# Gathering the tokens of two expert pairs at once, in two fp32r passes of 256 columns, with 19 prefetch buffers

## The chip, the cores and the metric

The kernel runs on one core of a Trainium2 chip. The metric is the device time of one execution in microseconds; the runs of a kernel are summarised by their median. The core has a matrix engine (TensorE, here PE; its weight loads are PEld), a vector engine (VectorE, DVE), a scalar engine (ScalarE, ACT), GpSimd (POOL) and SyncE (SP), which here issues the large loads. Matmuls write to eight accumulator banks of 512 fp32 columns.

## The reference

A transformer block with adaptive normalisation, latent and neighbourhood attention and a hierarchical mixture of experts is followed by a second block (gating, linear attention with decay, convolutional feed-forward). There are 256 tokens of width 1024. What the change touches is the mixture of experts: 16 experts in 4 groups; each token takes the best group and two experts in it. The reference computes all experts densely:

```python
def hierarchical_moe(h, w_rg, b_rg, w_re, b_re, w_gate, w_up, w_down):
    ...
    def one_group(args):
        wg_g, wu_g, wd_g, comb_g = args
        hid = jax.nn.silu(jnp.einsum('td,edf->tef', t, wg_g)) * jnp.einsum('td,edf->tef', t, wu_g)
        return jnp.einsum('tef,efd->td', hid * comb_g[:, :, None], wd_g)
```

with `w_gate` and `w_up` of 1024 x 512 and `w_down` of 512 x 1024 for each expert, all in fp32.

## The kernel before

The first block's attention comes first, then routing, then the expert loop, then the second block. In the expert part each expert takes at most 64 tokens (`CAP`), and two experts make a pair of 128 slots. Routing gives each chosen token a place in its expert; `slots_of(p)` (L984) compares places with slot numbers and makes the 0/1 matrix `SS[p]` (tokens x 128 slots, two halves of 128 tokens). `hT` (L950) is the normalised token matrix, tokens on partitions, written by ACT from the accumulator banks `tks`. `gather(p)` (L1058) multiplies `hT` by `SS[p]` in fp32, one 128-wide block of the model width at a time, into one bank per half of the width; `affine` (L1052) scales and shifts each block into `XE`, alternately on ACT and DVE.

The loop over 8 pairs (L1112) then runs, in this order on PE: the gate projection `pg` (L1121 and L1122, the two experts side by side), the transposes of `SS[p]` and the routing weights into a bank `aux` (L1131, L1133), the up projection `pu`, `combine` of the pair before (L1031 and L1032: its output times `ST` in fp32r, high and low part; DVE adds it to `X` at L1035), the transposes of the gated product (L1155, after DVE's multiply L1150), the gather of the next pair (L1064), and the down projection (L1167, L1168). ACT copies the transposed product back to SBUF (L1156) ahead of the down projection. `ST` (L1135) is the transposed slot matrix, copied by DVE out of `aux` right after the gate projection. PE runs in the order in which the program is written (`MANUAL`); the order on ACT, DVE and POOL is chosen by a planner when the kernel is built, within the dependencies that `follow` adds.

The experts' weights come as 96 chunks of 1 MB (1.0486 million bytes), 12 for a pair, two for each half of gate, up and down. `moe_next` (L831) takes them in order on SP's queue, and `KIND` gives each a buffer in turn: four of `rawp` (0), those of `big` (1), three of `bigB` (2), two of `wp` (3), one of `ho` (4); 21 in all. A load past the 21st waits for the matmuls that read the chunk 21 places earlier (`used`). `big` has 13 buffers; `mix` and `YY` take two of them. `mix` holds `XE`, the gated product `sgt` and both slot matrices. `overflow` (L1068) computes the experts again for tokens beyond 64 in an expert, in a conditional branch in the last pair. After the loop the second block's weights (`wC`) are loaded in the same queue, `raw0` first; `pre_high` (L1181) splits it into `wp` buffers.

Of the kernel before, what the change touches and what calls it, by code (L numbers as in the profile page):

```python
# [18 lines left out]
P = 128  # L19
D = 1024  # L20
KD = 8
T = 256
# [96 lines left out]
LAG = 2  # L119
DELAY_FROM = NF - 2  # L120
LASTCUT = 94
KIND = [1] * 9 + [0, 0, 1, 0, 0, 2, 2, 2, 3, 3, 4, 1]
FIRST = "m0 m1 w0 w3"
WARM = 30
EARLY = ("x0 j4 g0 x1 r0 c0 s0 h0 pA g1 j1 c1 h1 pB j3 A0 g2 A1 c2 h2 g3 B0 B1 c3 h3 A2 B2 pC g4 C0 C1 B3 c4 g5 h4 A3 C2 A4 c5 h5 B4 C3 g6 A5 c6 g7 h6 B5 C4 l0 A6 c7 h7 "
# [86 lines left out]
def build(tc, xT, cT, consts, constsA, constsZ, vec, wmod, wA, relb, wE, wC, sgw, sgb, sgln, gfin, out, dbg=None):  # L212
# [10 lines left out]
    with ExitStack() as top:  # L223
# [46 lines left out]
        def bank():  # L270
            return psp.tile([P, 512], F32, name=nm_("b"), tag="b")
# [7 lines left out]
        def follow(d, e):  # L279
            tc.add_manual_dep(d.ins, e.ins.name, order_only, reason="first things first")  # L280
# [84 lines left out]
        with ExitStack() as sa:  # L365
# [465 lines left out]
            def moe_next():  # L831
                i = moe_q[0]
                moe_q[0] += 1
                n = i - len(KIND)
                kind = KIND[i % len(KIND)]
                if kind == 0:
                    return load(moe_chunk(i), cuts=2 if i >= LASTCUT else 1)
                pl, tag = {1: (big, "raw"), 2: (bigB[-1], "raw"), 3: (wp, "w"), 4: (ho, "tL")}[kind]
                t = pl.tile([P, 2048], F32, name=nm_("raw"), tag=tag)
                for a, b in pieces(2048, 2 if i >= LASTCUT else 1):  # L840
                    d = queue(nc.sync.dma_start(t[:, a:b], moe_chunk(i)[:, a:b]))
                    tc.add_manual_dep(d.ins, (used[n] if n >= 0 else moe_gate[0]).ins.name, complete, reason="prefetch")
                return t
# [30 lines left out]
        br = pool(sb, "br", bufs=2)  # L874
        bigB.append(pool(sb, "bigB", bufs=3))
        mix = bigt([P, 2048], "mix")
        XE = mix[:, :KD * P].rearrange("p (k s) -> p k s", k=KD)
        sgt = mix[:, 1024:1536]
        warm(AF.Sqrt, lexp[0])
        G2 = bp.tile([P, KD], F32, name="G2")  # L880
# [44 lines left out]


        with sb:
            def small(shape, name, dt=F32):
                return bp.tile([P] + shape, dt, name=name)

            def bc(ap_, n):
                return ap_.unsqueeze(len(ap_.shape)).to_broadcast(list(ap_.shape) + [n])
# [14 lines left out]
            nc.vector.tensor_reduce(mx_, L, axis=AX.X, op=OP.max)  # L947
            nc.vector.tensor_sub(L, L, bc(mx_, 4))
            lexp[0] = nc.scalar.activation(ex, L, AF.Exp)
            hT = ho.tile([P, 2, D], F32, name="hT", tag="tH")  # L950
            for g in range(2):
                for b in range(2):
                    follow(nc.scalar.activation(hT[:, b, g * 512:(g + 1) * 512], tks[g, b], AF.Copy, scale=col[:, b:b + 1]), lexp[0])
            e1 = small([2, 5, 4], "e1")
            nc.vector.scalar_tensor_tensor(e1, L, 0.0, prio, op0=OP.is_ge, op1=OP.mult)
            nc.vector.tensor_reduce(mx_, e1, axis=AX.X, op=OP.max)
# [24 lines left out]
            slot = cst("slot")  # L981
            SS = {}

            def slots_of(p):  # L984
                SS[p] = mix[:, 1536 + p % 2 * 256:1792 + p % 2 * 256].rearrange("p (b e s) -> p b e s", b=2, e=2)
                for b in range(2):
                    nc.vector.tensor_tensor(SS[p][:, b], bc(place[:, b, 2 * p:2 * p + 2], CAP),
                                            slot.unsqueeze(1).to_broadcast([P, 2, CAP]), op=OP.is_equal)
                SS[p] = SS[p].rearrange("p b e s -> p b (e s)")

            slots_of(0)
            comb = small([2, 4, 4], "comb")
            nc.vector.tensor_mul(comb, exe, top)
            den = small([2, 5], "den")
# [60 lines left out]
                else:  # L1055
                    nc.scalar.activation(dst, src, AF.Identity, scale=G2[:, k:k + 1], bias=mod2[:, 8 + k:9 + k])

            def gather(p):  # L1058
                for g in range(2):
                    ps = bank()  # L1060
                    for k in range(4):
                        for b in range(2):
                            d = (4 * g + k) * P
                            mm(ps[:, k * P:(k + 1) * P], hT[:, b, d:d + P], SS[p][:, b], start=b == 0, stop=b == 1)  # L1064
                    for k in range(4):
                        affine(XE[:, 4 * g + k], ps[:, k * P:(k + 1) * P], 4 * g + k, k % 2)

            def overflow():  # L1068
                last[0] = None
                with tc.If(n_most > CAP):  # L1070
                    ob, turns = [bank() for _ in range(4)], itertools.count()
                    spare = [bigB[-1].tile([P, 2048], F32, name=f"spare{c}", tag="raw") for c in range(3)]
                    H2f, fw = spare[0].rearrange("p (k t) -> p k t", k=KD), spare[1:]
                    for k in range(KD):
                        ps = ob[next(turns) % 4]
                        for b in range(2):
                            nc.tensor.transpose(ps[:, b * P:(b + 1) * P], hT[:, b, k * P:(k + 1) * P], ident)
                        affine(H2f[:, k], ps[:, :T], k, False)
                    hc = bigt([P, 5, T], "hc")
                    hid, cr = hc[:, 0:4], hc[:, 4]  # L1080
                    with tc.For_i(0, NE, 1) as e:
                        nc.gpsimd.dma_start(cr, ovD[bass.ds(e, 1)].to_broadcast([P, T]))

                        def dload(c):
                            t = fw[c % 2]
                            nc.sync.dma_start(t, wE[bass.ds(e, 1), c].rearrange("o p n -> p (o n)"))
                            return t
                        wg = [dload(0), dload(1)]
                        for f in range(4):
                            pg = ob[next(turns) % 4]  # L1090
                            for k in range(KD):
                                s = slice((k % 4) * 512 + f * P, (k % 4) * 512 + (f + 1) * P)
                                mm(pg[:, :T], wg[k // 4][:, s], H2f[:, k], start=k == 0, stop=k == KD - 1)
                            nc.scalar.activation(hid[:, f], pg[:, :T], AF.Silu)
                        wu = [dload(2), dload(3)]
                        for f in range(4):
                            pu = ob[next(turns) % 4]
                            for k in range(KD):
                                s = slice((k % 4) * 512 + f * P, (k % 4) * 512 + (f + 1) * P)
                                mm(pu[:, :T], wu[k // 4][:, s], H2f[:, k], start=k == 0, stop=k == KD - 1)  # L1100
                            nc.vector.tensor_mul(hid[:, f], hid[:, f], pu[:, :T])
# [10 lines left out]
            for p in range(8):  # L1112
                def pairmm(ps, between=None):
                    for hf in range(2):
                        if hf and between:
                            between()
                        wa, wb = next_pair()
                        for kk in range(4):
                            k = 4 * hf + kk
                            s = slice(kk * 512, (kk + 1) * 512)  # L1120
                            la = mm(ps[0:64], XE[:, k, 0:64], wa[:, s], start=k == 0, stop=k == KD - 1)  # L1121
                            lb = mm(ps[64:128], XE[:, k, 64:128], wb[:, s], start=k == 0, stop=k == KD - 1)  # L1122
                        freed(la, lb)

                if p == 1:
# [2 lines left out]
                pairmm(pg, overflow if p == 7 else None)  # L1128
                aux = bank()
                for b in range(2):  # L1130
                    nc.tensor.transpose(aux[:, b * P:(b + 1) * P], SS[p][:, b], ident)  # L1131
                for b in range(2):
                    mm(aux[:, 256:272], SS[p][:, b], comb[:, b], start=b == 0, stop=b == 1)  # L1133
                ST = br.tile([P, T], F32R, name=f"ST{p}", tag="ST")
                nc.vector.tensor_copy(ST, aux[:, :T])  # L1135
                wt = br.tile([P, 1], F32, name=f"wt{p}", tag="wt")
                nc.vector.tensor_copy(wt[0:64], aux[0:64, 256 + 2 * p:257 + 2 * p])
                nc.vector.tensor_copy(wt[64:128], aux[64:128, 257 + 2 * p:258 + 2 * p])
# [3 lines left out]
                pairmm(pu)  # L1142
                if 0 < p < 7:
                    combine(*pend)
                sg = sgt
                nc.scalar.activation(sg, pg, AF.Silu)
                hd = sgt.rearrange("p (f t) -> p f t", f=4)
# [3 lines left out]
                for hf in range(2):  # L1151
# [2 lines left out]
                    for i in range(2):  # L1154
                        nc.tensor.transpose(pt[:, i * P:(i + 1) * P], hd[:, 2 * hf + i], ident)  # L1155
                    nc.scalar.copy(sg[:, o], pt)  # L1156
                if p < 7:
                    slots_of(p + 1)
                    gather(p + 1)
                pd = [bank(), bank()]  # L1160
                for hf in range(2):
                    wa, wb = next_pair()
# [490 lines left out]
```

## Time and profile before

| | us |
|---|---|
| median of 3 runs | 783.11 (781.49 to 783.50) |
| the profiled execution | 783.37 |
| its span | 781.7 |
| PE busy | 761.0 (97%) |
| DVE busy | 452.0 (58%) |
| ACT busy | 359.1 (46%) |
| POOL busy | 28.2 (4%) |

The span is the time from the first to the last instruction of the profiled execution; all times on the time axis below count from its start. Busy time is the union of an engine's instructions; PE's ends are modelled, so that starts are the better measure of spacing. An idle time is followed by what ended it, after an arrow. An fp32 matmul stands as two rows, an fp32r matmul as one.

### The profile page before, as it was taken

The page shows a single profiled execution, that of the slowest core. Times are in us where ns is not written, and L with a number is a line of the kernel's source. Part 1 is how long each engine was busy: PE and PEld are TensorE (multiplying, and loading weights), DVE is VectorE, ACT ScalarE, POOL GpSimd, SP SyncE. Part 2 cuts the span into 40 slices and gives each one's busy share as a digit, 9 for nine tenths or more (in the row PEclk, how much of TensorE's full clock was granted, in tenths as well). Part 3 has the DMA queues.
Part 4 walks back from the last instruction along what each step waited for, and adds up shares of the span by engine and source line. Part 5 has one row for each costly group of instructions (what it writes and reads, how often), then busy time and mean ns, then how long its engine had stood idle before and what let it go on. Part 6 is the DMA issues. An engine that isn't in the chain of part 4 may idle for free. (4 is left out here: it accounts for less than half of the span.)

```text
span 781.7 us, 12585 instructions
## 1 busy us (share of the span) xinstructions
PE 761.0 (97%) x5036; PEld 562.5 (72%) x5036; DVE 452.0 (58%) x926; ACT 359.1 (46%) x669; POOL 28.2 (4%) x35
## 2 busy tenths in 40 slices
PE   8999998999999999999999999999999999999996
PEld 7678776766789445535535535898899999999995
DVE  3737639865763123313313336887786877777785
ACT  5527345765663211111102106578766655655654
POOL 0001000000001000000000004103000000000000
PEclk9999999999999999999999999999999999999999
DMA  8867646657959899999999927654443555545301
GB/s 355 339 241 151 254 151 240 232 192 270 419 178 353 346 413 421 419 420 420 420 419 419 415 105 270 231 171 153 135 156 134 200 180 213 199 166 212 109 1 54
DMA packets 29343, 198.86 MB, mean 254 GB/s; under 512 B 3457, under 2 KB 3857, under 8 KB 6369
## 3 DMA queue, kind: packets, MB, share of 16 engines
q1 hardware_dynamic: 28224, 194.45, 64.5%
q0 software_dynamic: 1056, 3.56, 2.0%
q8 instruction: 41, 0.67, 0.4%
q14 instruction: 22, 0.17, 0.1%
HBM read 196.94 MB, written 1.06 MB: 253 GB/s over the span
## 5 line engine op out<-in xcount | busy, mean ns | idle before, releaser
L315 DVE TENSOR_TENSOR w<-raw,w 128x1024 fp32r<-128x1024 f32 (+1 forms) x118 | 140.0, 1213 | 31.3 <-ACT w L314 31.0
L314 ACT CAST w<-raw 128x1024 fp32r<-128x1024 f32 (+1 forms) x118 | 116.5, 1029 | 25.0 <-PE b L336 20.8
L1122 PE MATMUL b<-raw,mix 128*64 128x512 f32 x256 | 113.4, 594 | 0.5 <-issue 0.5
L1121 PE MATMUL b<-raw,mix 128*64 128x512 f32 x256 | 113.4, 594 | 0.3 <-PEq L1070 0.3
L334 PE MATMUL b<-fH,w 128*128 128x256 f32 x352 | 98.7, 280 | 0.0
L336 PE MATMUL b<-fH,w 128*128 128x256 f32 x352 | 98.3, 279 | 0.0
L335 PE MATMUL b<-fL,w 128*128 128x256 f32 x352 | 98.3, 279 | 0.0
L1121 PEld LDWEIGHTS b<-raw,mix 128*64 128x64 f32 x256 | 34.1, 137 | 67.0 <-issue 64.9
L334 PEld LDWEIGHTS b<-fH,w 128*128 128x128 f32 x352 | 66.1, 188 | 0.9
L335 PEld LDWEIGHTS b<-fL,w 128*128 128x128 f32 x352 | 65.9, 187 | 0.9
L336 PEld LDWEIGHTS b<-fH,w 128*128 128x128 f32 x352 | 66.1, 188 | 0.0
L1167 PE MATMUL b<-raw,mix 128*64 128x512 f32 x128 | 56.6, 595 | 0.0
L1168 PE MATMUL b<-raw,mix 128*64 128x512 f32 x128 | 56.6, 595 | 0.0
L1576 ACT ACTIVATE a<-t,V 128x256 f32<-128x256 f32 x44 | 26.3, 599 | 39.0 <-DVE t L1575 38.9
L1167 PEld LDWEIGHTS b<-raw,mix 128*64 128x64 f32 x128 | 16.9, 137 | 33.1 <-issue 32.0
L1156 ACT COPY mix<-b 128x256 f32<-128x256 f32 x16 | 5.4, 374 | 73.5 <-PE b L1155 73.3
L1122 PEld LDWEIGHTS b<-raw,mix 128*64 128x64 f32 x256 | 34.2, 137 | 2.8 <-issue 2.8
L1150 DVE SCALAR_TENSOR_TENSOR mix<-mix,wt,b 128x256 f32<-128x256 f32 x16 | 7.0, 477 | 48.4 <-PE b L1122 43.2
L336 PE MATMUL b<-w,mL 128*128 128x512 f32 x88 | 34.7, 395 | 0.0
L335 PE MATMUL b<-w,mH 128*128 128x512 f32 x88 | 34.7, 394 | 0.0
L334 PE MATMUL b<-w,mH 128*128 128x512 f32 x88 | 34.7, 394 | 0.0
L1172 DVE TENSOR_TENSOR YY<-b,YY 128x512 fp32r<-128x512 f32 x16 | 10.9, 689 | 38.9 <-ACT YY L1172 38.3
(429 smaller groups left out, 1702.5 us busy)
## 6 DMA issues: line engine op xcount, KB each, us to landing
raw<-in_wE SPq DMA_DIRECT2D x94, 1024.0 KB, 14.0
raw<-in_wC SPq DMA_DIRECT2D x46, 1024.0 KB, 4.9
raw<-in_wmod SPq DMA_DIRECT2D x24, 1024.0 KB, 6.8
raw<-in_wA SPq DMA_DIRECT2D x13, 1024.0 KB, 5.0
raw<-in_wE SPq DMA_DIRECT2D x4, 512.0 KB, 17.7
raw<-in_wA SPq DMA_DIRECT2D x2, 576.0 KB, 4.7
X<-in_xT SPq DMA_DIRECT2D x1, 1024.0 KB, 5.2
CX<-in_cT SPq DMA_DIRECT2D x1, 1024.0 KB, 7.4
```

The source lines that it names most:

```text
L314: hc = nc.scalar.copy(h[:, : b - a], raw[:, a:b])
L315: after[0] = (on or nc.vector).tensor_sub(l[:, : b - a], raw[:, a:b], h[:, : b - a])
L334: mm(ps, ah, bh, start=start, stop=False)
L335: mm(ps, ah, bl, start=False, stop=False)
L336: mm(ps, al, bh, start=False, stop=stop)
L1121: la = mm(ps[0:64], XE[:, k, 0:64], wa[:, s], start=k == 0, stop=k == KD - 1)
L1122: lb = mm(ps[64:128], XE[:, k, 64:128], wb[:, s], start=k == 0, stop=k == KD - 1)
L1150: nc.vector.scalar_tensor_tensor(sg[:, o], sg[:, o], wt, pu[:, o], op0=OP.mult, op1=OP.mult)
L1167: la = mm(pd[n][0:64], hd[:, f, 0:64], wa[:, s], start=f == 0, stop=f == 3)
L1168: lb = mm(pd[n][64:128], hd[:, f, 64:128], wb[:, s], start=f == 0, stop=f == 3)
L1172: ylast = (nc.scalar.copy(yH[:, o], pd[n]), nc.vector.tensor_sub(yL[:, o], pd[n], yH[:, o]))
L1576: nc.scalar.activation(a, t, AF.Identity, bias=bcv[:, n:n + 1], scale=wcv[:, 2, n:n + 1])
```

## The change

`hT` is replaced by two fp32r tiles: `hTH`, the rounded high part (ACT, as `hT` before), and `hTL`, the remainder, made by four DVE operations behind the first slot matrix; `hTL` takes the `ho` buffer that was a prefetch buffer. `slots_of` makes the matrix of two pairs at once (256 slots) in a tile of its own with one buffer, as fp32r. `gather` runs ahead of the loop and in pairs 1, 3 and 5 only; it multiplies the high and then the low part by 256 slots, into two banks per half of the width. `XE` becomes a tile of its own, twice as wide, in `big`. `ST` has one buffer instead of two, and its copy moves behind `combine`. The small fp32 tiles of routing move into the freed part of `mix`. `KIND` loses its last two entries, and so there are 19 prefetch buffers. In `overflow` the spare buffers come from `big`, and the two parts are added up first.

```diff
-KIND = [1] * 9 + [0, 0, 1, 0, 0, 2, 2, 2, 3, 3, 4, 1]
+KIND = [1] * 9 + [0, 0, 1, 0, 0, 2, 2, 2, 3, 3]
...
-        XE = mix[:, :KD * P].rearrange("p (k s) -> p k s", k=KD)
+        XE = bigt([P, KD, 2 * P], "XE")
...
-            hT = ho.tile([P, 2, D], F32, name="hT", tag="tH")
+            hTH = ho.tile([P, 2, D], F32R, name="hTH", tag="tH")
+            hTL = ho.tile([P, 2, D], F32R, name="hTL", tag="tL")
             for g in range(2):
                 for b in range(2):
-                    follow(nc.scalar.activation(hT[:, b, g * 512:(g + 1) * 512], tks[g, b], AF.Copy, scale=col[:, b:b + 1]), lexp[0])
+                    follow(nc.scalar.activation(hTH[:, b, g * 512:(g + 1) * 512], tks[g, b], AF.Copy, scale=col[:, b:b + 1]), lexp[0])
...
-            def slots_of(p):
-                SS[p] = mix[:, 1536 + p % 2 * 256:1792 + p % 2 * 256].rearrange("p (b e s) -> p b e s", b=2, e=2)
+            def slots_of(pp):
+                st = br.tile([P, 512], F32R, name=f"SS{pp}", tag="SS", bufs=1)
+                SS[pp] = st.bitcast(F32).rearrange("p (b s) -> p b s", b=2), st.rearrange("p (b s) -> p b s", b=2)
                 for b in range(2):
-                    nc.vector.tensor_tensor(SS[p][:, b], bc(place[:, b, 2 * p:2 * p + 2], CAP),
-                                            slot.unsqueeze(1).to_broadcast([P, 2, CAP]), op=OP.is_equal)
-                SS[p] = SS[p].rearrange("p b e s -> p b (e s)")
-
-            slots_of(0)
+                    d = nc.vector.tensor_tensor(SS[pp][1][:, b].rearrange("p (e s) -> p e s", e=4), bc(place[:, b, 4 * pp:4 * pp + 4], CAP),
+                                                slot.unsqueeze(1).to_broadcast([P, 4, CAP]), op=OP.is_equal)
+                return d
+
+            placed = slots_of(0)
+            for g in range(2):
+                for b in range(2):
+                    o = slice(g * 512, (g + 1) * 512)
+                    d = nc.vector.scalar_tensor_tensor(hTL[:, b, o], tks[g, b], col[:, b:b + 1], hTH[:, b, o], op0=OP.mult, op1=OP.subtract)
+                    follow(d, placed)
+                    placed = d
...
-            def gather(p):
+            def gather(pp):
                 for g in range(2):
-                    ps = bank()
-                    for k in range(4):
-                        for b in range(2):
-                            d = (4 * g + k) * P
-                            mm(ps[:, k * P:(k + 1) * P], hT[:, b, d:d + P], SS[p][:, b], start=b == 0, stop=b == 1)
-                    for k in range(4):
-                        affine(XE[:, 4 * g + k], ps[:, k * P:(k + 1) * P], 4 * g + k, k % 2)
+                    pss = [bank(), bank()]
+                    for i, ht in enumerate((hTH, hTL)):
+                        for j in range(4):
+                            for b in range(2):
+                                d = (4 * g + j) * P
+                                mm(pss[j // 2][:, (j % 2) * 256:(j % 2 + 1) * 256], ht[:, b, d:d + P], SS[pp][1][:, b],
+                                   start=i + j % 2 + b == 0, stop=i + j % 2 + b == 3)
+                    for j in range(4):
+                        affine(XE[:, 4 * g + j], pss[j // 2][:, (j % 2) * 256:(j % 2 + 1) * 256], 4 * g + j, j % 2)
...
-                ST = br.tile([P, T], F32R, name=f"ST{p}", tag="ST")
-                nc.vector.tensor_copy(ST, aux[:, :T])
...
                 if 0 < p < 7:
                     combine(*pend)
+                ST = br.tile([P, T], F32R, name=f"ST{p}", tag="ST", bufs=1)
+                nc.vector.tensor_copy(ST, aux[:, :T])
...
-                if p < 7:
-                    slots_of(p + 1)
-                    gather(p + 1)
+                if p % 2 and p < 7:
+                    slots_of(p // 2 + 1)
+                    gather(p // 2 + 1)
```

## Rows read from the trace of the kernel before

**Rows 1.** The page: busy time, share of the span and instructions of PE and PEld.

```profile
PE 761.0 (97%) x5036; PEld 562.5 (72%) x5036; DVE 452.0 (58%) x926; ACT 359.1 (46%) x669; POOL 28.2 (4%) x35
```

**Rows 2.** Windows: stretch, busy time by engine (instructions), PE clock, DMA share, GB/s.

```profile
283.30:311.10 27.80, 27.80 (x157) 13.47 (x158) 8.57 (x25) 4.08 (x9) 0.52 (x1) 1.00 1.01 421
...
422.10:449.80 27.70, 27.70 (x156) 13.36 (x154) 7.63 (x20) 4.24 (x9) 0.00 (x0) 1.00 1.01 416
...
476.90:490.00 13.10, 11.65 (x77) 9.83 (x78) 12.93 (x20) 12.85 (x29) 9.39 (x11) 1.00 0.78 287
```

**Rows 3.** Loads of line 841 at 259 to 260 and at 435.8: starts, landing.

```profile
L841 SPq DMA_DIRECT2D raw<-in_wE x2: 328/352/377, 259.3 to 259.7; - x2
...
DMA to landing us min/median/max: 4.9/6.6/8.4
...
L841 SPq DMA_DIRECT2D raw<-in_wE x1: 328/328/328, 435.8 to 435.8; - x1
...
DMA to landing us min/median/max: 16.0/16.0/16.0
```

**Rows 4.** Timeline of PE, last pair: start, duration, line, operation, tiles, shapes.

```profile
468.89 0.89 PE L1155 MATMUL b<-C,mix 128*128 128x128 f32 x4 [0.64 <-DVE mix L1150]
469.79 0.64 PE L1167 MATMUL b<-raw,mix 128*64 128x512 f32 x1
...
473.27 0.59 PE L1167 MATMUL b<-raw,mix 128*64 128x512 f32 x1
...
476.81 0.38 PE L1031 MATMUL b<-ST,YY 128*128 128x256 f32 x1
```

**Rows 5.** Timeline of PE, pair 0, transposes to down projection.

```profile
271.09 0.89 PE L1155 MATMUL b<-C,mix 128*128 128x128 f32 x4 [0.68 <-DVE mix L1150]
271.82 3.74 PE L1064 MATMUL b<-mix,hT 128*128 128x128 f32 x32
275.49 0.64 PE L1167 MATMUL b<-raw,mix 128*64 128x512 f32 x1
```

**Rows 6.** Timeline of all engines, pair 6, slot copy and combine to down projection.

```profile
429.85 0.43 DVE L1135 CAST ST<-b 128x256 fp32r<-128x256 f32 x1 [6.24 <-PE b L1133]
...
436.76 0.38 PE L1031 MATMUL b<-ST,YY 128*128 128x256 f32 x1
...
437.75 3.22 DVE L1035 SCALAR_TENSOR_TENSOR X<-b,mod,X 128x256 f32<-128x256 f32 x8
...
438.67 0.28 PE L1032 MATMUL b<-ST,YY 128*128 128x256 f32 x1
...
438.78 0.60 PE L1155 MATMUL b<-C,mix 128*128 128x128 f32 x4
...
439.20 0.65 ACT L1156 COPY mix<-b 128x256 f32<-128x256 f32 x2 [9.38 <-PE b L1155]
...
442.89 0.64 PE L1167 MATMUL b<-raw,mix 128*64 128x512 f32 x1
```

**Rows 7.** Timeline of all engines around the gather ahead of the loop.

```profile
247.22 2.40 ACT L953 ACTIVATE hT<-b,colB 128x512 f32<-128x512 f32 x4
...
251.41 0.49 DVE L987 TENSOR_TENSOR mix<-place,C 128x128 f32<-128x128 f32 x2
...
251.85 3.81 PE L1064 MATMUL b<-mix,hT 128*128 128x128 f32 x32 [0.70 <-DVE mix L987]
...
255.59 0.64 PE L1121 MATMUL b<-raw,mix 128*64 128x512 f32 x1
```

**Rows 8.** The page's groups: count, busy us, mean ns, idle before, releaser.

```profile
L1156 ACT COPY mix<-b 128x256 f32<-128x256 f32 x16 | 5.4, 374 | 73.5 <-PE b L1155 73.3
...
L1172 DVE TENSOR_TENSOR YY<-b,YY 128x512 fp32r<-128x512 f32 x16 | 10.9, 689 | 38.9 <-ACT YY L1172 38.3
```

**Rows 9.** Waits from 476.9 to the end: who for whom, us, times, longest.

```profile
ACT w L314 <- PE b L336: 8.5, 7, 1.8
```

More of the change, by code (lines that the diff above doesn't have):

```diff
@@ L837, in moe_next @@
                     return load(moe_chunk(i), cuts=2 if i >= LASTCUT else 1)
-                pl, tag = {1: (big, "raw"), 2: (bigB[-1], "raw"), 3: (wp, "w"), 4: (ho, "tL")}[kind]
+                pl, tag = {1: (big, "raw"), 2: (bigB[-1], "raw"), 3: (wp, "w")}[kind]
                 t = pl.tile([P, 2048], F32, name=nm_("raw"), tag=tag)
@@ L927, in build @@
         with sb:
+            taken = [1536]
             def small(shape, name, dt=F32):
-                return bp.tile([P] + shape, dt, name=name)
+                if dt != F32:
+                    return bp.tile([P] + shape, dt, name=name)
+                taken[0] += math.prod(shape)
+                assert taken[0] <= 2048
+                names = "abc"[:len(shape)]
+                return mix[:, taken[0] - math.prod(shape):taken[0]].rearrange(f"p ({' '.join(names)}) -> p {' '.join(names)}", **dict(zip(names[:-1], shape)))
             def bc(ap_, n):
@@ L1071, in overflow @@
                     ob, turns = [bank() for _ in range(4)], itertools.count()
-                    spare = [bigB[-1].tile([P, 2048], F32, name=f"spare{c}", tag="raw") for c in range(3)]
+                    spare = [bigt([P, 2048], f"spare{c}") for c in range(3)]
                     H2f, fw = spare[0].rearrange("p (k t) -> p k t", k=KD), spare[1:]
+                    hR = fw[0].rearrange("p (b d) -> p b d", b=2)
+                    nc.vector.tensor_add(hR, hTH, hTL)
                     for k in range(KD):
@@ L1076, in overflow @@
                         for b in range(2):
-                            nc.tensor.transpose(ps[:, b * P:(b + 1) * P], hT[:, b, k * P:(k + 1) * P], ident)
+                            nc.tensor.transpose(ps[:, b * P:(b + 1) * P], hR[:, b, k * P:(k + 1) * P], ident)
                         affine(H2f[:, k], ps[:, :T], k, False)
@@ L1112, in build @@
             for p in range(8):
+                x = p % 2 * P
+                ss = SS[p // 2][0][:, :, x:x + P]
                 def pairmm(ps, between=None):
@@ L1120, in pairmm @@
                             s = slice(kk * 512, (kk + 1) * 512)
-                            la = mm(ps[0:64], XE[:, k, 0:64], wa[:, s], start=k == 0, stop=k == KD - 1)
-                            lb = mm(ps[64:128], XE[:, k, 64:128], wb[:, s], start=k == 0, stop=k == KD - 1)
+                            la = mm(ps[0:64], XE[:, k, x:x + 64], wa[:, s], start=k == 0, stop=k == KD - 1)
+                            lb = mm(ps[64:128], XE[:, k, x + 64:x + 128], wb[:, s], start=k == 0, stop=k == KD - 1)
                         freed(la, lb)
@@ L1130, in build @@
                 for b in range(2):
-                    nc.tensor.transpose(aux[:, b * P:(b + 1) * P], SS[p][:, b], ident)
+                    nc.tensor.transpose(aux[:, b * P:(b + 1) * P], ss[:, b], ident)
                 for b in range(2):
-                    mm(aux[:, 256:272], SS[p][:, b], comb[:, b], start=b == 0, stop=b == 1)
-                ST = br.tile([P, T], F32R, name=f"ST{p}", tag="ST")
-                nc.vector.tensor_copy(ST, aux[:, :T])
+                    mm(aux[:, 256:272], ss[:, b], comb[:, b], start=b == 0, stop=b == 1)
                 wt = br.tile([P, 1], F32, name=f"wt{p}", tag="wt")
```

## The prediction

> **What bounds the kernel now.** I read the page first, then the windows by stage, the timeline at the seams of the expert loop, and the loads. TensorE (PE) is busy for 97% of the span [rows 1], so the question is which of its work the change removes and what stands ready to stop it when it is early. The windows show the expert loop: each pair of experts takes 27.7 to 27.8 us with PE busy throughout (pairs 2 to 5 read the same as pairs 1 and 6), and in the same stretches the loads run at a DMA share of 1.00 to 1.01 and 416 to 421 GB/s [rows 2]. Two resources are full at once; which of them ends the stage is read at its end: the last load, issued at 435.8, lands 16.0 us later, at 451.8 [rows 3], and the last half of the last down-projection starts at 473.27 [rows 4]. So the loads lead by 21.5 us there, PE ends the stage, and what PE saves counts until that lead is used up. A pair needs 12 chunks of 1.0486 MB = 12.58 MB, 30.0 us at 420 GB/s, against 27.7 us of PE: the lead shrinks already now by 2.3 us a pair.
>
> **The gather itself.** Now each of 8 gathers issues 32 matmuls (16 fp32 products, two rows each) in 3.74 us [rows 5], 3.67 from its first start to the down-projection's. After it, 4 gathers issue 2 passes x 8 blocks x 2 token halves = 32 matmuls of 128x256 in fp32r. The nearest row is the same form, combine: sixteen matmuls with a new weight each start from 436.76 to 438.67, 0.127 us apart, the first gap of 0.22 included, 0.12 otherwise [rows 6]. So a gather of two pairs costs 32 x 0.121 = 3.9 us, 0.2 more than one of one pair now. Bounds: 3.7 (no first gap) and 4.1 (0.127 throughout). The sum of the busy time, 8 x 3.67 - 4 x 3.9 = 13.8 us, isn't the gain: the gather also covers waits, so I go through its places.
>
> **Pair 0's gather, ahead of the loop.** Now PE starts on it at 251.85 and the expert matmuls at 255.59 [rows 7]. Three things are added. The slot comparison is twice as wide: the two of 128 columns take 0.49 us, and I take 0.76, the second ending at 252.3 (the change reads both token halves in turn, so PE starts in earnest there). The high pass of four blocks, 8 x 0.12 = 1.0, ends at 253.3. The low pass needs hTL, four VectorE (DVE) subtractions of 512 columns out of the accumulators, queued behind the slots; the nearest row, the same size and sources, is 0.689 us each [rows 8]. The first two end at about 253.7, so PE waits 0.4 us once; the other two end at 255.1, under the second half's high pass. Then 253.7 + 3 x 0.96 = 256.6, less what runs while waiting: I take 256.5, 0.9 us later than now (bounds 0.5, if the waits overlap, and 2.0, if small routing operations get between them on DVE). Queued behind the four subtractions on DVE are the rest of the routing and the odd blocks' affine; the first expert matmul needs only block 0, which ScalarE (ACT) writes. The high half is written by the same four ACT instructions as now, done by 249.6 [rows 7].
>
> **Pairs without a gather.** After an even pair's up-projection the down-projection follows the four transposes directly. In pair 0 transposes to down-projection take 275.49 - 271.09 = 4.40 [rows 5]; the last pair, which has no gather today, shows what is left: 469.79 - 468.89 = 0.90 [rows 4]. Saved: 3.5. In pairs 2, 4 and 6 combine has already covered the multiply ahead of the transposes; now it is 442.89 - 438.78 = 4.11, and what remains is the transposes and one of the two ACT copies, which starts at 439.20 and takes 0.374 [rows 6, 8]: down-projection at 439.65, so 3.24 saved each, 9.7 in all (bounds 3.0 and 3.5 each). Here the gather's cover is gone, and 0.3 us of waiting for ACT is priced in.
>
> **Pairs 1, 3 and 5** pay 0.2 each, 0.6. Their slots are now in one buffer instead of two, free once the odd pair's transposes have read it, some 8 us ahead of the gather; nothing there. The affine of 256 columns instead of 128 has the 7.0 us of the down-projection (469.79 to 476.81) [rows 4] to finish in; nothing. Sum: 0.9 - 3.5 - 9.7 + 0.6 = -11.7 us, the loop's end at 476.8 - 11.7 = 465.1.
>
> **The loads.** There are 19 prefetch buffers for 21: the one in ho (now hTL) and one of big (now XE) are given up. Now the first load that has to wait for a buffer is chunk 21, issued at 259.3 as pair 0's first half is used up, and it lands 4.9 us later [rows 3]; the 75 chunks from there take 75 x 1.0486 / 420 = 187.2 us, and 259.3 + 4.9 + 187.2 = 451.4 meets the landing read above. After it, chunk 19 waits for the same event at 260.2, and 77 chunks take 192.2: the last lands at 457.3. SP's queue is in order, so all later loads stand behind chunk 19. The last half's matmuls are due at 473.27 - 11.7 = 461.6. The lead falls from 21.5 to 4.3 us, but stays positive: the price is nothing, with a bound of 2 us for a start half a chunk or so worse. Earlier leads are larger, since PE gains on the loads pair by pair.
>
> The loads of the loop move 416 to 421 GB/s with all engines full [rows 2]. The Trainium skill, "Perfetto Trace Analysis", section Roofline, bounds one core's 16 DMA engines at about 435 GB/s, which speaks against giving up buffers: what isn't prefetched can't be caught up. By that figure 77 chunks would take 185.6 us (an estimate from that page), the lead would be 10.9, and the second case below would drop out; the trace shows the lower rate, and it decides.
>
> **What follows the loop.** From 476.9 to 490 PE waits on ACT, DVE and GpSimd, which are all busy (12.85, 12.93 and 9.39 of 13.10 us) [rows 2], and later the splitting of weights waits for PE to free buffers [rows 9]: neither hangs on loads, so the rest should shift as a block. The new order of kinds puts chunks 93 and 94 in the wp buffers that the next block's first split takes; they are free at the loop's end, where that split is queued today. The weight loads behind the experts' (raw0, then wC 1, 3, 4) find their buffers sooner; raw0 would land at 457.3 + 2.5 = 459.8, ahead of 465.1. The small routing tiles only change their place, and the edits of overflow lie in a branch that isn't entered. Nothing gained or lost; I allow 2 us either way, since ACT's and DVE's order may differ.
>
> **How the numbers follow.** The profiled execution took 783.37 us, 781.7 of it span, 0.26 above the median of 783.11. Span 781.7 - 11.7 = 770.0; from the median, 771.4.
> - The forecast: 771.4 (own range 769 to 774), 0.70.
> - The loads take the end: if the stream stands two to four chunks (5 to 10 us) worse at 260 than reckoned, PE waits 0.7 to 5.7 us in the last down-projection: about 775. For it: a lead of only 4.3. Against it: the sum meets today's landing within 0.4. Chance 0.10.
> - A smaller loss on PE: the copy of ST is moved behind combine and has one buffer, so it runs on DVE after the eight updates that end at 440.97 [rows 6], and takes 0.43, until 441.4. If the accumulator bank it frees is the one that the down-projection takes next, each of pairs 2, 4 and 6 waits 441.4 - 439.65 = 1.8 us: 5.3, so 776.7. Against it: eight banks, and the up-projection's comes free as the updates begin, combine's first soon after [rows 6]. Behind that copy on DVE stand an odd pair's affines, which nobody needs for 7 us. Chance 0.10.
> - The other side: the same copy, if its bank is wanted already by the transposes at 438.78. Then all of pairs 1 to 6 wait 441.4 - 438.78 = 2.6 us, 15.7 in all, 4.0 more than the gain: 787.1. It decides from 1.95 us a pair (11.7 / 6). Against it: up to there a pair asks for no more than eight banks (gate's, aux, up, four of combine, and the gate's is long free). Chance 0.04; with the down-projection and the gathers waiting instead, no change, 0.04.
> - The passes don't run as combine's rows do: at the 0.23 us that a 128-column fp32 product costs, doubled for 256 columns, a gather is 14.7 us, four of them 59 against 29.4, so some 800. The fp32r rows speak against it: 0.02.
>
> Range: 768 to 778, which takes in the bounds above (start up to 1.1 worse, passes 0.8, rest 2), the loads' and the smaller loss. Within 0.3%, 780.8 to 785.5, is about what a measurement of this kernel can't tell from no change. Faster 0.90 (the first three cases), same 0.04, slower 0.06.
>
> **What would show it.** Right: 32 matmuls of 256 columns in some 3.9 us per gather, four times; expert matmuls from 256.3 to 257; in pairs 0, 2, 4 and 6 the down-projection within 1.0 us of the transposes; the loop's end near 465; the last expert load landing at 457 to 458, with its issue no longer held by a buffer; no wait of PE on an expert load. Wrong: a wait of the last halves on raw<-in_wE (the loads bind), transposes or down-projections that wait for DVE's ST copy (the banks), a first expert matmul after 258, or a loop's end at 465 with a total that doesn't follow it (the block behind it changed).

## The result and the profile after

The changed kernel takes 771.2 us (median of 5 runs, 770.63 to 772.56), the kernel before 782.54 (5 runs beside it, 781.49 to 783.5): a ratio of 0.9861, 95% interval 0.985 to 0.9872. That is 11.3 us less; the span of the profiled execution fell by 12.1 us, from 781.7 to 769.6. The forecast was 771.4, within 768 to 778.

The page of the kernel after, busy time of the engines; 761.0 us of TensorE (PE) in [rows 1] became 748.6, with 128 matmuls fewer:

```profile
PE 748.6 (97%) x4908; PEld 549.5 (71%) x4908; DVE 448.7 (58%) x906; ACT 353.2 (46%) x653; POOL 28.2 (4%) x35
```

Windows of after, with the columns of [rows 2]: pairs 1, 2 and 6, each from its first expert matmul to the next pair's, and the 13.1 us behind the loop:

```profile
280.60:309.00 28.40, 28.36 (x157) 13.65 (x158) 9.15 (x25) 4.47 (x9) 0.52 (x1) 1.00 1.01 422
309.00:333.40 24.40, 24.16 (x124) 9.74 (x122) 6.00 (x15) 2.42 (x5) 0.00 (x0) 1.00 1.01 419
...
413.70:438.20 24.50, 24.26 (x126) 9.80 (x124) 6.09 (x16) 2.42 (x5) 0.00 (x0) 1.00 1.01 420
...
464.70:477.80 13.10, 11.61 (x78) 9.78 (x77) 12.93 (x20) 12.78 (x29) 9.31 (x10) 1.00 0.86 325
```

The even pairs are 3.3 us shorter than the 27.7 to 27.8 of [rows 2], the odd ones hardly longer, pair 1 most. The DMA share is as full as it was, at the same GB/s. The stretch behind the loop has the busy times it had [rows 2]: it has moved as a block. From the loop's end to the end of the span it is 304.9 us in both (781.7 - 476.8 [rows 4] and 769.6 - 464.7).

Timeline of PE at the seams of after: start, duration, line, operation, tiles, shapes, idle before. First pair 0 from the transposes to the down-projection, then pair 5 (transposes, the gather of pairs 6 and 7), then pair 6:

```profile
271.94 0.83 PE L1177 MATMUL b<-C,mix 128*128 128x128 f32 x4 [0.67 <-DVE mix L1172]
272.83 0.64 PE L1189 MATMUL b<-raw,mix 128*64 128x512 f32 x1
...
402.51 0.60 PE L1177 MATMUL b<-C,mix 128*128 128x128 f32 x4
402.86 1.18 PE L1080 MATMUL b<-SS,hTH 128*128 128x256 f32 x8
403.88 1.10 PE L1080 MATMUL b<-SS,hTL 128*128 128x256 f32 x8
404.82 1.10 PE L1080 MATMUL b<-SS,hTH 128*128 128x256 f32 x8
405.76 1.10 PE L1080 MATMUL b<-SS,hTL 128*128 128x256 f32 x8
...
430.39 0.60 PE L1177 MATMUL b<-C,mix 128*128 128x128 f32 x4
431.23 0.64 PE L1189 MATMUL b<-raw,mix 128*64 128x512 f32 x1 [0.24 <-ACT mix L1178]
```

In pair 5, 24 matmuls start in 405.76 - 402.86 = 2.90 us, 0.121 apart with the first gap in: the gather is the 3.9 us of the forecast. In pairs 0 and 6 the gather is gone, and ahead of pair 6's down-projection the 0.24 us wait for ScalarE's (ACT) copy has come into the open.

The last load of the experts in after, issue and landing, beside [rows 3]:

```profile
L841 SPq DMA_DIRECT2D raw<-in_wE x1: 328/328/328, 440.4 to 440.4; - x1
...
DMA to landing us min/median/max: 16.5/16.5/16.5
```

It lands at 440.4 + 16.5 = 456.9, and the last half of the down-projection starts here:

```profile
461.15 0.59 PE L1189 MATMUL b<-raw,mix 128*64 128x512 f32 x1
```

So the lead is 461.1 - 456.9 = 4.2 us, where it was 21.5 [rows 3, 4]. The waits of PE in after's loop name no load.

Where the 12.1 us at the loop's end (476.8 to 464.7) came from, by the starts of the pairs' first matmuls in the two timelines: 0.85 later at the first, pair 0 3.5 shorter, pairs 2, 4 and 6 3.3 each (9.9 by their sum), pairs 1, 3 and 5 longer by 0.57, 0.18 and 0.15 (0.9 by their sum), pair 7 shorter by 0.5. Pair 7's share lies around the branch of `overflow`, where PE stood for 0.8 us before and 0.4 after; the prediction had no term for it.

### The profile page after: what moved, and what is told of

Same layout as the page of the kernel before. It is cut to its first block, busy times and chain, and to the rows that moved or that the text cites. A ratio compares the mean times of both kernels' runs of the same rounds, so it can differ in the third digit from the quotient of the medians.

```text
span 769.6 us, 12285 instructions
## 1 busy us (share of the span) xinstructions
PE 748.6 (97%) x4908; PEld 549.5 (71%) x4908; DVE 448.7 (58%) x906; ACT 353.2 (46%) x653; POOL 28.2 (4%) x35
## 5 line engine op out<-in xcount | busy, mean ns | idle before, releaser
L1143 PE MATMUL b<-raw,XE 128*64 128x512 f32 x256 | 113.4, 594 | 0.4 <-issue 0.2
L1144 PE MATMUL b<-raw,XE 128*64 128x512 f32 x256 | 113.4, 594 | 0.0
L1143 PEld LDWEIGHTS b<-raw,XE 128*64 128x64 f32 x256 | 34.1, 137 | 69.0 <-issue 67.1
L1189 PE MATMUL b<-raw,mix 128*64 128x512 f32 x128 | 56.6, 595 | 0.8 <-ACT mix L1178 0.7
L1190 PE MATMUL b<-raw,mix 128*64 128x512 f32 x128 | 56.6, 595 | 0.0
L1189 PEld LDWEIGHTS b<-raw,mix 128*64 128x64 f32 x128 | 16.9, 137 | 34.4 <-issue 32.0
L1144 PEld LDWEIGHTS b<-raw,XE 128*64 128x64 f32 x256 | 34.1, 137 | 0.3 <-issue 0.3
```

What stands on the lines that cost most here:

```text
L1143: la = mm(ps[0:64], XE[:, k, x:x + 64], wa[:, s], start=k == 0, stop=k == KD - 1)
L1144: lb = mm(ps[64:128], XE[:, k, x + 64:x + 128], wb[:, s], start=k == 0, stop=k == KD - 1)
L1189: la = mm(pd[n][0:64], hd[:, f, 0:64], wa[:, s], start=f == 0, stop=f == 3)
L1190: lb = mm(pd[n][64:128], hd[:, f, 64:128], wb[:, s], start=f == 0, stop=f == 3)
```

## The experiments

**The shallower prefetch alone.** In the kernel before, a load waits for the half that stands 19 loads earlier:

```diff
-                n = i - len(KIND)
+                n = i - 19
...
-        ready.extend(moe_next() for _ in range(len(KIND) - moe_q[0]))
+        ready.extend(moe_next() for _ in range(19 - moe_q[0]))
```

> The kernel before, with nothing changed but the depth of the prefetch: a load waits for the release of the half that stands 19 loads earlier instead of 21; the gather is the old one. Theory (TensorE's own work sets the end of the expert loop, the loads have a lead): the last half's load lands 2 x 2.50 = 5.0 us later against its use, the lead of 21.5 us falls to about 16.5, and the time stays at 782.5 us (+-0.6). Rival (the loads, or the buffers that they wait for, already decide somewhere in the loop): up to 5.0 us slower, 787.5 us, with matmuls that wait for a load.

Measured: 782.03 us, ratio 0.9992 (0.9983 to 1.0002). Its last load, with issue and landing, and the start of the last half:

```profile
L841 SPq DMA_DIRECT2D raw<-in_wE x1: 328/328/328, 445.7 to 445.7; - x1
...
DMA to landing us min/median/max: 13.5/13.5/13.5
```

```profile
473.14 0.59 PE L1167 MATMUL b<-raw,mix 128*64 128x512 f32 x1
```

The load lands at 459.2, the lead at the last half is 473.1 - 459.2 = 13.9, 2.6 less than expected (the halves ahead of it have 18.4 and 18.9), and the time doesn't change. The two buffers cost nothing while PE had its old work.

**The pairing alone.** Two pairs in one fp32 pass:

```diff
-            hTH = ho.tile([P, 2, D], F32R, name="hTH", tag="tH")
-            hTL = ho.tile([P, 2, D], F32R, name="hTL", tag="tL")
+            hTH = ho.tile([P, 2, D], F32, name="hTH", tag="tH")
...
-                    for i, ht in enumerate((hTH, hTL)):
+                    for i, ht in enumerate((hTH,)):
...
```

> The kernel after, but the two pairs are gathered in one fp32 pass of 256 columns; the rounded-off low part and its VectorE work are gone, since fp32 needs none. 16 products of 256 columns per gather. Theory (a product's cost goes with its columns and with the two rows that fp32 takes): the warm-up products of 128x256 fp32 took 1.89 us for 8 rows, 0.236 each, so a gather is 32 x 0.236 = 7.6 us for two pairs against 2 x 3.67 = 7.3 before; the four gathers together cost what the eight did, the loop gains only the seams, and the time is 780 to 784 us. Rival (what costs is the number of products and weight loads, so pairing by itself halves it): 3.7 us per gather, four times 3.6 us saved, about 768 us, no more than the kernel after.

**The fp32r passes alone.** One pair at a time, 128 columns:

```diff
-                                mm(pss[j // 2][:, (j % 2) * 256:(j % 2 + 1) * 256], ht[:, b, d:d + P], SS[pp][1][:, b],
+                                mm(ps[:, j * P:(j + 1) * P], ht[:, b, d:d + P], SS[pp][1][:, b, y:y + P],
...
-                if p % 2 and p < 7:
-                    slots_of(p // 2 + 1)
-                    gather(p // 2 + 1)
+                if p % 2 and p < 7:
+                    slots_of(p // 2 + 1)
+                if p < 7:
+                    gather(p + 1)
```

> The kernel after, but each pair is gathered by itself: two fp32r passes of 128 columns, 32 matmuls per pair, eight gathers. Theory (the pairing is what makes fp32r pay): a matmul of 128 columns costs no less than the 0.114 us of a 128-column fp32 row, so a gather is 32 x 0.114 = 3.65 us as before, the eight cost 29 us, and the time is near that of before, 780 to 785 us; if a narrow fp32r matmul is slower than that, up to the 0.229 us of a whole 128-column fp32 product, the eight cost 58.6 us and the time is up to 811 us. Rival (the cost goes with the columns at fp32r's rate, 0.06 us): 1.94 us per pair, together the same as in the kernel after, about 771 us, and the pairing was not needed.

Measured: the pairing alone 783.19 us, ratio 1.0011 (0.9997 to 1.0025); the passes alone 785.65, ratio 1.004 (1.0019 to 1.006). Timeline of PE, first the gather in pair 1 of the pairing alone (32 rows of fp32), then the one in pair 1 of the passes alone:

```profile
301.19 7.07 PE L1073 MATMUL b<-SS,hTH 128*128 128x256 f32 x32
```

```profile
300.90 1.09 PE L1081 MATMUL b<-SS,hTH 128*128 128x128 f32 x8
301.83 1.06 PE L1081 MATMUL b<-SS,hTL 128*128 128x128 f32 x8
302.72 1.06 PE L1081 MATMUL b<-SS,hTH 128*128 128x128 f32 x8
303.61 1.06 PE L1081 MATMUL b<-SS,hTL 128*128 128x128 f32 x8
```

Neither half of the change is worth anything by itself, as both theories had it. The pairing alone does shorten the loop, from 221.2 to 217.6 us, but its first gather, 7.1 us long where one pair takes 3.7, stands ahead of the loop, which starts 3.8 us later (259.4 for 255.6). An fp32 matmul of 256 columns costs 7.07 / 32 = 0.221 us, twice the 0.114 of one of 128, so pairing in fp32 moves the same cost about. An fp32r matmul of 128 columns starts every (303.61 - 300.90) / 24 = 0.113 us, and one of 256 every 0.121: the second 128 columns are nearly free, and only who uses them gains. That the weights set this floor is supported by fp32 matmuls of a single column with 128 columns of new weights, in after at a granted clock of 1.00:

```profile
244.06 0.36 PE L913 MATMUL b<-ones,mix 128*128 128x1 f32 x2
244.28 0.36 PE L914 MATMUL b<-ones,mix 128*128 128x1 f32 x2
```

They start every 0.22 / 2 = 0.11 us, with next to nothing to multiply. Whether an fp32r matmul of 128 columns would be quicker with fewer weights to load, no run here shows. The Trainium skill, "TensorE: Matmul & The Clock Gate", section LDWEIGHTS, puts a weight load at P / 1.2 ns for P columns, an estimate of 107 ns for 128. The 0.11 us of these rows and the 0.113 of the fp32r ones lie just above it.

The profiled execution of the passes alone has a span of 781.2, that of before 781.7. Its timed runs lie 781.21 to 789.58 apart, the longer ones at a lower mean granted clock (0.996 at the shortest, 0.983 at the longest); the 3 us by which its median is above before come from there, and why that kernel's clock is granted less in many runs isn't settled.

**The late slot copy alone,** in the kernel before:

```diff
-                ST = br.tile([P, T], F32R, name=f"ST{p}", tag="ST")
-                nc.vector.tensor_copy(ST, aux[:, :T])
...
                 if 0 < p < 7:
                     combine(*pend)
+                ST = br.tile([P, T], F32R, name=f"ST{p}", tag="ST")
+                nc.vector.tensor_copy(ST, aux[:, :T])
```

> The kernel before with one edit of the change alone: VectorE's copy of the transposed slots stands behind the second projection and the combine instead of right behind the transposes, so its bank of sums is held some 10 us longer in every pair. Theory (a bank is still free when the next step wants one, and the copy of 0.43 us lies beside other work): 782.5 us (+-0.6). Rival 1 (the held bank stops TensorE at the transposes, which then wait for the copy): some 0.55 us in each of eight pairs, up to 787 us. Rival 2 (the copy came at a bad moment before and its removal shortens the seam): up to 0.4 us gained in each pair, 779 to 780 us.

Measured: 782.59 us, ratio 1.0001 (0.999 to 1.0011). This run says nothing about the copy: its trace has it at 428.82 in pair 6, where it was, since with two buffers the recorded order could put it back. So it was run again with `bufs=1` on ST, as in the change:

> The kernel before with this edit of the change alone, and with the single buffer that the change gives ST: in the run without that, the recorded order had put the copy back to its old place (428.82 us in pair 6, ahead of the second projection). With one buffer it can only stand behind the combine. Its bank of sums is held some 10 us longer in every pair, with all eight gathers in place. Theory (no one is short of a bank, and VectorE has room): 782.4 us (+-0.6), no wait of TensorE on the copy. Rival (the prediction's other side: the transposes or the gather find no bank): up to 2.6 us in each of pairs 1 to 6, up to 798 us, with TensorE waiting on the copy's line.

Measured: 781.82 us, ratio 0.9992 (0.9977 to 1.0006). Timeline of VectorE (DVE) in its pair 6:

```profile
437.90 3.22 DVE L1035 SCALAR_TENSOR_TENSOR X<-b,mod,X 128x256 f32<-128x256 f32 x8
441.04 0.41 DVE L1144 CAST ST<-b 128x256 fp32r<-128x256 f32 x1
```

The copy ends at 441.45, as the rival had priced it (441.4), and nobody waits for it: PE's waits in the loop are those of before. Both rivals that hang on its bank fall.

**How much lead there is.** The kernel after with a load that waits for the half 17 and 15 loads earlier (the edit is that of the first experiment, with these numbers):

> The kernel after, but a load waits for the release of the half 17 loads earlier instead of 19. Theory (the loads come back to back at 2.50 us a chunk once the first half is released, so two buffers fewer put every later load 5.0 us later, and the lead of 4.2 us at the last half is all there is): the lead becomes 4.2 - 5.0 = -0.8 us, TensorE waits for loads near the end, and the time is about 0.8 us over that of after, 772.0 us. Rival (the loads make up lost time, since the stretches in which they wait for a release take up the 5.0 us): 771.2 us, and the lead at the end stays over 2 us.

> The kernel after with the prefetch cut to 15 loads. Theory: the lead of 4.2 us minus 4 x 2.50 us is -5.8 us, so the loop ends 5.8 us later and the time is 777.0 us; TensorE's waits for loads sum to about 5.8 us. Rival (the lead is made up again in the loop): 771.2 to 772.5 us.

Measured: 774.91 us at 17, ratio 0.9895 (0.9877 to 0.9913); 775.21 at 15, ratio 0.9917 (0.9893 to 0.9941). At 15 the loop is 212.7 us long against 208.3 in after, 4.4 more, and PE waits for loads in pair 7 (the waits of PE in the loop; us, times, longest; then a row of the timeline with the longer wait, in the gate projection):

```profile
PE b L1144 <- DMA raw<-in_wE: 2.3, 2, 1.6
```

```profile
445.38 0.64 PE L1144 MATMUL b<-raw,XE 128*64 128x512 f32 x1 [1.63 <-DMA raw<-in_wE]
```

The named waits are 2.3 of the 4.4 us. The 4.4 lie in pairs 6 (0.5) and 7 (3.9), where the loads of three halves land 0.4, 1.6 and 2.6 us after the half's first matmul.

At 17 the loop is 2.4 us longer, without such a wait, and that fits neither theory. Its waits of PE have one that after has shorter, 1.3 us in two places:

```profile
PE b L1177 <- DVE mix L1172: 3.9, 3, 2.6
```

It stands in pair 1. Timelines of DVE there, after's and then that of the run at 17:

```profile
296.17 0.88 DVE L1050 SCALAR_TENSOR_TENSOR X<-b,mod,X 128x256 f32<-128x256 f32 x2 [6.58 <-PE b L1047]
296.96 0.86 DVE L1172 SCALAR_TENSOR_TENSOR mix<-mix,wt,b 128x256 f32<-128x256 f32 x2
297.74 2.43 DVE L1050 SCALAR_TENSOR_TENSOR X<-b,mod,X 128x256 f32<-128x256 f32 x6
```

```profile
297.72 3.23 DVE L1050 SCALAR_TENSOR_TENSOR X<-b,mod,X 128x256 f32<-128x256 f32 x8 [6.57 <-PE b L1047]
300.86 0.41 DVE L1166 CAST ST<-b 128x256 fp32r<-128x256 f32 x1
301.19 0.86 DVE L1172 SCALAR_TENSOR_TENSOR mix<-mix,wt,b 128x256 f32<-128x256 f32 x2
```

The products of line 1172, which the transposes wait for, stand behind all of combine's eight updates at 17, behind two in after, and ahead of them in pairs 2 to 6 of either (the two expectations below count one and four). The order of DVE was not edited; it came out different in that kernel. Pair 1's seam, from the up-projection's last half to the down-projection, is 12.9 us there, 10.2 in after, 9.8 in pairs 3 and 5. So the order was fixed by hand, at 19 and at 17 loads:

```diff
-                if 0 < p < 7:
-                    combine(*pend)
-                ST = br.tile([P, T], F32R, name=f"ST{p}", tag="ST", bufs=1)
-                nc.vector.tensor_copy(ST, aux[:, :T])
...
-                    nc.vector.scalar_tensor_tensor(sg[:, o], sg[:, o], wt, pu[:, o], op0=OP.mult, op1=OP.mult)
+                    prod = nc.vector.scalar_tensor_tensor(sg[:, o], sg[:, o], wt, pu[:, o], op0=OP.mult, op1=OP.mult)
+                if 0 < p < 7:
+                    combine(*pend, then=lambda mi, e: follow(e, prod))
+                ST = br.tile([P, T], F32R, name=f"ST{p}", tag="ST", bufs=1)
+                follow(nc.vector.tensor_copy(ST, aux[:, :T]), prod)
```

> The kernel after with VectorE's order fixed by hand in every pair: the two products that the transposes wait for (L1168 here) stand ahead of the combine's additions and of the slot copy, as the kernel before has them and as pairs 2 to 6 of after have them; in pair 1 of after one addition stands between them. Theory (this order is what makes pair 1's seam 10.2 us where those of pairs 3 and 5 are 9.8): pair 1's seam becomes 9.8 us and the time 770.8 us (+-0.6). Rival (pair 1 is longer for its own work, the late part of the routing): its seam stays 10.2 us, time 771.2 us. The traces' seam tells these apart, the time does not.

> The same with loads 17 deep instead of 19. In the first run of this depth VectorE had another order in pair 1 (four additions of the combine ahead of the last product), and that pair's seam was 12.9 us. Theory (the order, and not the depth, cost those 2.7 us; a depth of 17 only takes the loads' lead of 4.2 us to about -0.7 us, and the run at 15 shows a last half that starts at -1.2 us): pair 1's seam 9.8 us, the loop 207.9 us long, time 770.8 us (+-0.8). Rival (the depth itself costs, through later loads): seam or last pairs longer by 2 to 4 us, 773 to 775 us.

Measured: 770.45 us at 19, ratio 0.9859 (0.9842 to 0.9876), and 770.3 at 17, ratio 0.9862 (0.984 to 0.9885). Pair 1's seam is 9.8 us in both, and the loop is 207.7 and 207.8 us long. The 17-deep run's last load and the start of its last half:

```profile
L841 SPq DMA_DIRECT2D raw<-in_wE x1: 328/328/328, 445.9 to 445.9; - x1
...
DMA to landing us min/median/max: 15.2/15.2/15.2
```

```profile
459.91 0.59 PE L1189 MATMUL b<-raw,mix 128*64 128x512 f32 x1
```

The load lands at 461.1, 1.2 us after the half that uses it has begun, and costs nothing: the last chunks are loaded in two pieces, the half begins on the first, and the second is first multiplied at 461.6. So at least 4.2 + 1.2 = 5.4 us of lead can be spent there. In the run at 15 the last half again begins 1.2 us ahead of its landing: its loads end 9.8 us later against the first release (206.6 for 196.8 us), of which the lead took 5.4 and the loop lost the other 4.4. That is a balance of one trace and no second proof of the 5.4. With the order fixed the loop is 0.5 us shorter than after's 208.3; the time of 770.45 us can't be told from after's.

**The high pass alone.** The part of the tokens below fp32r's digits is left out:

```diff
-            hTL = ho.tile([P, 2, D], F32R, name="hTL", tag="tL")
...
-                    for i, ht in enumerate((hTH, hTL)):
+                    for i, ht in enumerate((hTH,)):
...
```

> The kernel after without the low part: one fp32r pass of 256 columns gathers two pairs, so the part of the tokens below fp32r's digits is left out of what the experts get. Theory (the loads take over as soon as their lead is used up): TensorE's work falls by 16 x 0.121 = 1.9 us in each of the three gathers in the loop, 5.8 us, and by 1.9 to 2.9 us in the one ahead of it, which also releases the first half earlier; of the 5.8 us only the lead of 4.2 us can be had, so the time is 6.1 to 7.1 us below after, 764.1 to 765.1 us, and the last halves wait about 1.6 us for loads. Rival (TensorE still decides): 7.7 to 8.7 us below, 762.5 to 763.5 us, without such waits.

Measured: 765.86 us, ratio 0.9782 (0.9765 to 0.98). The loop is 203.4 us long, 4.8 less than in after, and the last half starts 0.3 us ahead of its load, within what may be spent. No load is waited for. The odd pairs' seams fell by 1.9 each, 5.6 together; 0.8 came back in pair 7, where PE's own sequencer holds it at the branch:

```profile
PE b L1136 <- PEq L1080: 1.8, 1, 1.8
```

So the loads did not take over, and the theory's reason was wrong: with at least 5.4 us to spend, and not 4.2, there was room for nearly all of it. The size doesn't decide: 5.3 us below after by the medians, 7.7 by the spans. Why the branch takes 1.8 us here and 0.2 in after is open; in the run with the warm-ups below, whose loads are those of after, it takes 2.0.

**The clock ahead of the loop.** In the profile of after the first expert matmul starts 5.68 us after the first gather does, where the forecast has 256.5 - 251.85 = 4.65. Timeline of PE, then windows, with the granted clock in the third column from the end:

```profile
250.76 2.09 PE L1080 MATMUL b<-SS,hTH 128*128 128x256 f32 x8 [0.90 <-DVE SS L996]
252.65 1.91 PE L1080 MATMUL b<-SS,hTL 128*128 128x256 f32 x8
254.36 1.22 PE L1080 MATMUL b<-SS,hTH 128*128 128x256 f32 x8
255.41 1.10 PE L1080 MATMUL b<-SS,hTL 128*128 128x256 f32 x8
256.44 0.64 PE L1143 MATMUL b<-raw,XE 128*64 128x512 f32 x1
```

```profile
250.00:252.00 2.00, 1.24 (x5) 1.12 (x6) 1.97 (x6) 0.00 (x0) 0.00 (x0) 0.80 0.98 414
252.00:254.00 2.00, 2.00 (x11) 2.00 (x11) 1.66 (x4) 0.26 (x1) 0.00 (x0) 0.50 0.08 33
254.00:256.00 2.00, 2.00 (x17) 2.00 (x16) 1.28 (x4) 0.88 (x2) 0.00 (x0) 0.85 0.00 0
```

The clock was at its lower level, 1.2 GHz, through the first half of the gather. The kernel before had such a stretch in its own profile, earlier:

```profile
246.00:248.00 2.00, 2.00 (x14) 2.00 (x13) 1.70 (x10) 1.99 (x5) 0.00 (x0) 0.67 1.01 418
248.00:250.00 2.00, 2.00 (x6) 1.55 (x6) 1.73 (x10) 1.62 (x3) 0.00 (x0) 0.50 1.03 430
```

There it lay on the warm-up matmuls of the routing. To see whether the idle 0.39 and 0.90 us ahead of after's gather bring it, they were filled:

```diff
-WARM_R = 4
+WARM_R = 5
...
             place = small([2, 16], "place")
+            for k in range(2):
+                mm(rk[:, T:2 * T], ones, acc2, start=True, stop=True)
```

> The kernel after with three more warm-up products of 256 columns around the ranking: five instead of four ahead of it, and two between the ranking and the first gather, where TensorE was idle for 0.39 and 0.90 us. In the kernel after the granted clock is at half for about 3.5 us from 251.5 us on, in the first gather, which takes 5.68 us instead of 3.9. Theory (the idle time ahead of the gather brings the fall): with the gap filled the level stays at 1.00, the first expert matmul starts about 1.8 us earlier, at 254.6 us, and the time is 769.4 us. Rival (a stretch at half level comes about then whatever TensorE does; in the kernel before it came in windows in which TensorE was busy throughout): the stretch stays or moves by a microsecond, and the time is 771.2 us (+-0.5), as after.

Measured: 771.82 us, ratio 0.986 (0.9846 to 0.9874). In its profile the stretch at half lies at 246 to 252, ahead of the gap; and since `place` reads the bank that the two fillers write, DVE waited 1.91 us for them, so the edit has a cost of its own, and the gather was still preceded by 0.91 us of idle time. As a test of the gap it is inconclusive. The other runs settle it better: the runs at 15 and 17, the one with the high pass alone and both with the fixed order have the same idle gaps and a granted clock of 1.00 from 240 to 262. The gaps alone don't bring the fall.

## Why the prediction was right, point by point

**Gather, 3.9 us for two pairs:** right, by the rows of combine [rows 6]; 0.121 us apart, four gathers. The two experiments that split the change show that both halves of that reasoning are needed.

**Pair 0's gather, 0.9 later:** right, but the profile of after alone would not say so, since the stretch at half clock lay on the routing in one profile and on the gather in the other. Against the undisturbed timelines below it cost the routing of before some 1.0 us and the gather of after 1.2, which nearly cancel in the start (256.44 for 255.59). Two runs without it there give the term undisturbed. The timelines of PE from the ranking's last matmul to the first expert matmul, first in the kernel before (the run with the late copy, which moved nothing), then in the 15-deep run, whose gather is after's:

```profile
249.54 0.37 PE L978 MATMUL b<-sel,ones 128*128 128x16 f32 x2
250.62 3.81 PE L1064 MATMUL b<-mix,hT 128*128 128x128 f32 x32 [0.70 <-DVE mix L987]
254.36 0.64 PE L1121 MATMUL b<-raw,mix 128*64 128x512 f32 x1
```

```profile
249.21 0.37 PE L986 MATMUL b<-mix,ones 128*128 128x16 f32 x2
250.49 1.39 PE L1080 MATMUL b<-SS,hTH 128*128 128x256 f32 x8 [0.90 <-DVE SS L996]
251.72 1.43 PE L1080 MATMUL b<-SS,hTL 128*128 128x256 f32 x8
...
254.98 0.64 PE L1143 MATMUL b<-raw,XE 128*64 128x512 f32 x1
```

254.36 - 249.54 = 4.82 and 254.98 - 249.21 = 5.77: 0.95 more, for 0.9 forecast. The waits come otherwise than forecast, as some 0.3 us in each of the first two passes (251.72 - 250.49 = 1.23 us for the first, against 0.96) and not as 0.4 once.

**Pairs without a gather:** 3.5 in pair 0 (0.89 for 4.40 [rows 5]) and 3.27 in pair 6 (431.23 - 430.39 = 0.84 for 4.11 [rows 6]), forecast 3.5 and 3.24. The ACT copy that comes into the open is there, with 0.24.

**Pairs 1, 3 and 5, 0.2 each:** right for 3 and 5; pair 1 paid 0.6. The step that was missing is a term for DVE's order inside the loop, which the prediction allowed for only behind it: pair 1's products came to stand behind combine's first two updates on DVE, and fixing the order gave the 0.4 back. That this order came from the change's moved copy or its single buffer isn't shown. The sum came out near all the same by luck, since pair 7's 0.5, for which there was no term either, covers it. That 771.2 and 771.4 agree within 0.2 us is luck too: single executions of one kernel differ by about 2 us.

**The loads, lead 4.3 us:** 4.2 measured, last landing 456.9 for 457.3. The rate stayed where [rows 2] had it, at 419 to 422 GB/s. The higher figure of the Trainium skill ("Perfetto Trace Analysis", section Roofline), about 435 GB/s for one core's 16 DMA engines, was not reached. That a positive lead costs nothing is shown by the run at 17 with the fixed order, where even the last half's -1.2 us costs nothing. At least 5.4 us could be spent, 1.1 more than the prediction counted on, since it took a half to need all of its load at its start.

**The rivals:** banks held by the ST copy cost nothing, in the change and by themselves in the kernel before; passes at the fp32 rate did not come; the loads don't decide at a depth of 17 and do at 15. **The tail** shifted as a block, 304.9 us long in both.

## What to carry to other kernels

Where a matmul's columns no longer set its cost, because the weights must be loaded anyway, look for a second user of the same weights before a cheaper type: here either alone gave nothing and both together 11 us. Price a prefetch buffer by the lead at the last use, and count pieces that land while the first are already in use. After an edit, compare the order on the engines that wasn't meant to change: one seam differed by 2.7 us between two kernels of the same text but for a number.

## What the runs showed of the hardware

An fp32r matmul with new weights takes 0.113 us at 128 columns and 0.121 at 256; an fp32 one (two of which make a product) 0.114 and 0.221. The Trainium skill, "FP8 and Floating Point Precision", section TensorE Precision Notes, counts four passes for a true fp32 product. 2 x 0.221 us for 256 columns is 3.7 times the 0.121 of the one fp32r matmul, which roughly agrees.

The granted clock drops to half for 3 to 4 us at places that no edit here moved at will: all 13 profiles have one such stretch between 133 and 141 us and one at the very end of the span, and eight have another, three at 23 to 28 us and five between 246 and 255. Of 29 runs of the kernel before, timed beside the depth, the two halves of the change and the warm-ups, those with a mean granted clock of 0.996 took 781.23 to 782.68 us and those with 0.993 782.96 to 784.26. That goes with most of the spread of the timings, about 2 us, but not with all of it: beside other experiments two runs of the same kernel at 0.996 took 783.73 and 783.96. A difference of a microsecond between two single profiles says nothing until it is known where the stretch lay. What sets its place is open.
